# An expert stage that begins with the gather of its first pair alone

## The chip, the cores and the metric

The kernel runs on one core of one Trainium2 chip. The metric is the device time of one execution in microseconds (us); the median of a few runs counts. The core's engines are TensorE (PE; its weight loads are listed apart, as PEld), the vector engine (DVE), the scalar engine (ACT), GpSimd (POOL) and the sync engine (SP), whose queue issues nearly all loads from device memory.

## What is computed

Two transformer blocks of two layers each, on 256 rows of width 1024, in float32. The change touches the mixture of experts, which ends both layers of the first block. Cut to that:

```python
scores = sigmoid(einsum('nd,de->ne', h, router_w))
biased = (scores + router_bias).reshape(n, N_GROUPS, GROUP_SIZE)
group_sel = argmax(sum(top_k(biased, 2)[0], -1), -1)     # the best of 4 groups
...
_, idx = top_k(cand, TOP_K)                              # 2 of that group's 4 experts
sel = take_along_axis(scores, idx, -1)
gates = sel / sum(sel, -1, keepdims=True)
...
ffn = sum over experts e of gate_e * (silu(h @ w_gate[e]) * (h @ w_up[e])) @ w_down[e]
```

There are 16 experts of inner width 512. Each expert has three weight matrices of 2 MB, so a layer reads some 100 MB of expert weights.

## The kernel before

**Places.** The kernel gives each expert 64 places (`CAP`). After the router it counts for each row the place that it takes in each of its experts, and builds two masks `pm[t]` (one for each half `t` of the rows, 128 x 1024 in float32r): column 64 e + n is one for the row that has place n of expert e. The masks are made in two steps at L1246 to L1252, for experts 0 to 3 first.

**Gather.** `gather(g)` multiplies the rows, split into a high and a low float32r part (`hh`, `hl`), by 256 columns of the masks, that is by four experts or two pairs, and so brings the rows of those experts to their places, transposed: 8 blocks j x 2 halves t x 2 parts = 32 matmuls of 128 x 128 weights and 256 columns (L1284, L1285), two blocks to a PSUM bank, copied out by ACT and DVE (L1286, L1287) to the tile `m0` or `m1`.

**Pairs.** Experts are worked in eight pairs. For a pair, `gate_or_up` (L1315) multiplies its gathered rows by the gate and up weights: 16 plain float32 matmuls for each of the two experts and each of the two products; a plain float32 matmul appears in the trace as two passes. The two experts of a pair write the upper and the lower half of one bank, and run side by side. `act` (L1324, L1325) makes silu(gate) x up x the gate of the place, `tr` (L1331) transposes it behind the next pair's gate products, `down` (L1348) multiplies by the down weights, `scatter` (L1365) adds the result to the rows. Two transposes of short vectors for later layers (L683, L689) come in layer 0 at the start of pair 1.

**Gates of the places.** Before the pairs, 16 small matmuls (32 passes, L1296) bring each row's gate to its place, and two copies (L1300) put them into `gsl`, which `act` reads. Just ahead of them, `memory_gemm` (L1722) uses the waiting time of the router for a product of the second block.

**Banks.** Tiles of PSUM are named by tag: `mm` has three banks, `tp` one, and who takes one waits until the reader of the one before is done. L1296, L1331 and L683 all use `tp`.

**Loads.** `Stream` loads weights in one fixed order on SP's queue, 1 MB at a time, into 7 buffers `stage` and 6 `piece`, and a few free tiles ahead of time. A load is issued when its buffer has been released by the matmuls that read it (L141), and the queue keeps its order, so one load that waits holds up all behind it.

**Order.** Instructions of an engine run in the order in which a scheduler puts them: by the order of the code, moved where `after(...)` says that work is to be placed behind another instruction.

Of the kernel before, what the change touches and what calls it, by code (L numbers as in the profile page):

```python
# [9 lines left out]
F32 = mybir.dt.float32  # L10
F32R = mybir.dt.float32r
I32 = mybir.dt.int32
AF = mybir.ActivationFunctionType
# [3 lines left out]
P = 128  # L17
# [249 lines left out]
class Kern:  # L267
# [911 lines left out]
    def moe(self, l, res, ln):  # L1179
        nc, I, c, ws = self.nc, self.I, self.c, self.ws  # L1180
        n, hh, hl = ln.n, ln.hh, ln.hl
# [3 lines left out]
        p = self.tp()  # L1185
        for t in range(2):
            o = p[:, 16 * t:16 * t + 16]
# [13 lines left out]
        k = 0  # L1201
# [41 lines left out]
        nc.vector.scalar_tensor_tensor(posx, sel, -FAR, pp[:, 0:32], op0=OP.mult, op1=OP.add)  # L1243

        pm = [self.mp.tile([P, D], F32R, name="gv", tag="gv", bufs=2) for t in range(2)]
        for e0, e1 in ((0, 4), (4, 16)):  # L1246
            for t in range(2):
                at_pm = nc.vector.tensor_tensor(
                    pm[t][:, CAP * e0:CAP * e1].rearrange("p (e n) -> p e n", n=CAP),
                    c["slot"][:, None, 0:CAP].to_broadcast([P, e1 - e0, CAP]),  # L1250
                    posx[:, 16 * t + e0:16 * t + e1].rearrange("p (e o) -> p e o", o=1).to_broadcast([P, e1 - e0, CAP]),
                    op=OP.is_equal)  # L1252
        pos = self.sm(48, "gpos")
        nc.vector.tensor_copy(pos, pp[:, 0:48])

        gates = self.sm(32, "ggate")
# [14 lines left out]
        xg = []  # L1271
# [14 lines left out]
                nc.scalar.activation(x[:, j0, :], p[:, 0:256], AF.Copy)  # L1286
                nc.vector.tensor_copy(x[:, j0 + 1, :], p[:, 256:512])  # L1287

        gather(0)
        self.memory_gemm(l, 0, [self.prob()[:, 0:512] for t in range(2)], {7: [at_pp]})  # L1290

        p = self.tp()
        gsl = self.sm(8, "gsl")
        for pr in range(8):
            for t in range(2):
                nc.tensor.matmul(p[:, 2 * pr:2 * pr + 2], pm[t][:, P * pr:P * pr + P].bitcast(F32),  # L1296
                                 gates[:, 16 * t + 2 * pr:16 * t + 2 * pr + 2], start=(t == 0), stop=(t == 1))
        pv = p[:, 0:16].rearrange("p (a k) -> p a k", k=2)
        for k in range(2):
            nc.vector.tensor_copy(gsl[64 * k:64 * k + 64, :], pv[64 * k:64 * k + 64, :, k])  # L1300

        act_t, ptr = [], []

# [66 lines left out]
        state = {}  # L1370
        pend = None
        for pr in range(9):
            if pr == 4:
                more = nc.values_load(ovi[0:1, 0:1], min_val=0, max_val=1)
                with self.tc.If(more > 0):
                    self.moe_more(l, res, pos, gates, hh, hl, act_t[0][:, 1024:2048])
            if pr < 8:
                ga = gate_or_up("gate", pr)
            if pend is not None:
                with self.after(*([state["gate"]] if pr < 8 else [])):  # L1380
                    at = tr(pr - 1, pend)
            if pr == 2:
                ptr.append(self.slot("xl", F32R).rearrange("p (a n) -> p a n", a=8))
                for q in range(0, 8, 2):
                    p = self.mm()
                    for k in range(2):
                        for t in range(2):
                            nc.tensor.transpose(p[:, 256 * k + P * t:256 * k + P * t + P],
                                                pm[t][:, P * (q + k):P * (q + k) + P].bitcast(F32), c["ident"])
                    nc.scalar.activation(ptr[0][:, q:q + 2, :], p.rearrange("p (a n) -> p a n", a=2), AF.Copy)  # L1390
            with self.after(*([state["gate"]] if 1 < pr < 8 else [])):
                if pr in (3, 5):
                    gather(pr // 2 + 1)
                if pr > 1:
                    scatter(pr - 2, y)
            if pr < 8:
                ua = gate_or_up("up", pr)
            if pend is not None:
                y = down(pr - 1, at)
            if pr == 1:  # L1400
                with self.after(state["down"]):
                    gather(1)
            if pr < 8:
                pend = act(pr, ga, ua)
            else:
                nxt = LayerNorm(self, res, gb, ("xh", "xl"), self.gcol["ffn1_norm_2", 0] if l else None)
                scatter(7, y)
            if pr == 6:
                ws.hold("fgn" if l else "w_in")
            if pr == 0 and l == 0:  # L1410
                with self.after(at_act, at_pm):
                    self.gain_columns(1)
                    for _ in self.vectors(1):
                        pass
            if pr == 5:
                rows = self.spread_gb(I["ln2_g"], I["ln2_b"], l, "m2")
                next(rows)
            if pr == 6:
                gb = next(rows)
        m0 = self.slot("m0")  # L1420
# [11 lines left out]
        at = self.memory_gemm(l, 1, [m0[:, 512 * t:512 * t + 512] for t in range(2)], {0: [state["scatter"]]}, first, l)  # L1432
# [842 lines left out]
```

## Time and profile before

| | us |
|---|---|
| median of 3 runs | 1941.78 (1941.69 to 1943.78) |
| the profiled execution | 1940.31 |
| its span | 1938.5 |
| TensorE busy in the span | 1891.8 |
| expert products of layer 0 begin | 177.85 |
| expert products of layer 1 begin | 559.95 |

The span is the profiled execution from its first to its last instruction; all times in rows are counted from its start. In the table by stretches, a line gives the busy time of each engine in that stretch and in brackets the number of its instructions, then TensorE's granted clock (1.00 is full speed), the mean busy share of the 16 DMA engines (it can read slightly over 1) and the GB/s that they moved. In the timeline, a line is an instruction, or several of a kind that follow each other (x count), with start and length. Matmuls overlap, so their lengths don't add up: how long a row of matmuls takes is read from one start to the next.

### The profile page before, as it was taken

Reading aid. Unit: us, or ns where it says so; the run is one execution under the profiler, and the core shown is the slowest. Engines: PE = TensorE matmul, PEld = TensorE weight load, DVE = VectorE, ACT = ScalarE, POOL = GpSimd, SP = SyncE. Lnnn points to the kernel's source line nnn. Section 1 sums busy time; section 2 is a strip of 40 time slices with the busy share of each in tenths; the row PEclk is TensorE's granted clock in tenths of the full one; section 3 lists DMA queues with packets and bytes.
Section 4 is the critical chain, followed back from the end, with each engine's and each line's share of the span. In section 5 each row is a group of like instructions: output and inputs, shape, how many; then the busy total and the mean of one; then the engine's idle time right before and its main releaser. Section 6 shows DMA issues by size and latency. Waiting matters only on the chain.

```text
span 1938.5 us, 27919 instructions
## 1 busy us (share of the span) xinstructions
PE 1891.8 (98%) x11029; PEld 1449.2 (75%) x11029; DVE 1117.4 (58%) x2226; ACT 862.8 (45%) x1550; POOL 46.4 (2%) x93
## 2 busy tenths in 40 slices
PE   6999999999999999999999999999999999999999
PEld 6775444378754443799988988899899986788998
DVE  6875122277741223765579857555655568766554
ACT  5662111056521101654477656544644466656443
POOL 1010000000000000000001000000000000000000
PEclk9999999999999999999999999999999999999999
DMA  8568999964679999655553553555555553434550
GB/s 284 174 232 297 399 426 426 423 235 157 236 305 414 425 426 422 235 187 211 181 185 110 175 217 131 194 179 183 195 174 196 195 164 135 152 109 157 192 196 23
DMA packets 175211, 453.36 MB, mean 234 GB/s; under 512 B 10288, under 2 KB 106012, under 8 KB 148316
## 3 DMA queue, kind: packets, MB, share of 16 engines
q1 hardware_dynamic: 171212, 435.53, 60.2%
q0 software_dynamic: 3856, 15.91, 2.4%
q8 instruction: 91, 1.49, 0.3%
q14 instruction: 52, 0.43, 0.1%
HBM read 446.17 MB, written 5.24 MB: 233 GB/s over the span
## 4 chain that ended last, share of the span: by engine, by line
PE 60%; ACT 2%; DMA 2%; DVE 2%; issue 0%; POOL 0%; ACTq 0%; SPq 0%
PE mm L1588 8%; PE mm L1589 8%; PE mm L1587 8%; PE acca L487 5%; PE acca L488 5%; PE accb L486 4%; PE accb L487 4%; PE accb L488 4%; PE acca L486 4%; PE mm L1315 2%; DMA piece<-in_exp_w_down_dram 1%; DMA piece<-in_exp_w_gate_dram 1%; PE mm L1851 1%; PE acca L1348 1%; PE accb L1348 1%; PE mm L545 1%
## 5 line engine op out<-in xcount | busy, mean ns | idle before, releaser
L167 DVE TENSOR_TENSOR piece<-stage,piece 128x1024 fp32r<-128x1024 f32 (+3 forms) x439 | 513.5, 1179 | 238.2 <-ACT piece L166 236.6
L166 ACT ACTIVATE piece<-stage 128x1024 fp32r<-128x1024 f32 (+3 forms) x439 | 444.1, 1022 | 335.8 <-PE mm L1589 198.3
L1315 PE MATMUL mm<-stage,m 128*64 128x512 f32 x528 | 225.1, 595 | 2.4 <-DMA stage<-in_exp_w_gate_dram 2.4
L1315 PE MATMUL mm<-piece,m 128*64 128x512 f32 x480 | 213.4, 595 | 2.6 <-DMA piece<-in_exp_w_gate_dram 2.5
L1588 PE MATMUL mm<-m,piece 128*128 128x256 f32 x736 | 206.6, 281 | 0.0
L1587 PE MATMUL mm<-m,piece 128*128 128x256 f32 x736 | 206.2, 280 | 0.0
L1589 PE MATMUL mm<-m,piece 128*128 128x256 f32 x736 | 206.1, 280 | 0.0
L1587 PE MATMUL mm<-xh,piece 128*128 128x256 f32 x576 | 163.1, 283 | 0.0
L1589 PE MATMUL mm<-xh,piece 128*128 128x256 f32 x576 | 163.0, 283 | 0.0
L1588 PE MATMUL mm<-xl,piece 128*128 128x256 f32 x576 | 162.9, 283 | 0.0
L486 PE MATMUL accb<-piece,m 128*128 128x512 f32 (+1 forms) x364 | 143.2, 394 | 1.4 <-DVE res L1670 0.8
L487 PE MATMUL accb<-piece,m 128*128 128x512 f32 (+1 forms) x364 | 144.4, 397 | 0.0
L488 PE MATMUL accb<-piece,m 128*128 128x512 f32 (+1 forms) x364 | 144.2, 396 | 0.0
L1587 PEld LDWEIGHTS mm<-m,piece 128*128 128x128 f32 x736 | 138.4, 188 | 1.9 <-issue 0.3
L1588 PEld LDWEIGHTS mm<-m,piece 128*128 128x128 f32 x736 | 138.2, 188 | 1.6 <-issue 0.2
L1589 PEld LDWEIGHTS mm<-m,piece 128*128 128x128 f32 x736 | 138.7, 189 | 0.2 <-issue 0.2
L486 PE MATMUL acca<-piece,m 128*128 128x512 f32 (+1 forms) x348 | 137.3, 396 | 0.9 <-ACT m L496 0.8
L487 PE MATMUL acca<-piece,m 128*128 128x512 f32 (+1 forms) x348 | 137.8, 396 | 0.0
L488 PE MATMUL acca<-piece,m 128*128 128x512 f32 (+1 forms) x348 | 137.3, 395 | 0.0
L1315 PEld LDWEIGHTS mm<-stage,m 128*64 128x64 f32 x528 | 67.7, 137 | 82.9 <-issue 74.8
L1587 PEld LDWEIGHTS mm<-xh,piece 128*128 128x128 f32 x576 | 110.4, 192 | 1.3
L1588 PEld LDWEIGHTS mm<-xl,piece 128*128 128x128 f32 x576 | 110.4, 192 | 1.2
(572 smaller groups left out, 3480.2 us busy)
## 6 DMA issues: line engine op xcount, KB each, us to landing
stage<-in_ffn_wi_dram SPq DMA_DIRECT2D x88, 1024.0 KB, 5.1
stage<-in_ffn_wo_dram SPq DMA_DIRECT2D x44, 1024.0 KB, 5.1
stage<-in_exp_w_gate_dram SPq DMA_DIRECT2D x34, 1024.0 KB, 12.5
stage<-in_exp_w_down_dram SPq DMA_DIRECT2D x34, 1024.0 KB, 13.0
stage<-in_exp_w_up_dram SPq DMA_DIRECT2D x32, 1024.0 KB, 13.0
piece<-in_exp_w_gate_dram SPq DMA_DIRECT2D x30, 1024.0 KB, 10.6
piece<-in_exp_w_up_dram SPq DMA_DIRECT2D x30, 1024.0 KB, 11.0
piece<-in_exp_w_down_dram SPq DMA_DIRECT2D x24, 1024.0 KB, 19.5
```

The source lines that it names most:

```text
L166: nc.scalar.activation(wh, src, AF.Copy)
L167: nc.vector.tensor_tensor(wl, src, wh.bitcast(F32), op=OP.subtract)
L486: nc.tensor.matmul(out, ah, bh, start=first, stop=False)
L487: nc.tensor.matmul(out, ah, bl, start=False, stop=False)
L488: self.last_mm = nc.tensor.matmul(out, al, bh, start=False, stop=last)
L545: self.moved = nc.tensor.transpose(p[:, k * P:(k + 1) * P], src[:, 4 * q + k:D:8], self.c["ident"])
L1315: mm = nc.tensor.matmul(o[64 * k:64 * k + 64, :], x[:, j, s:s + CAP], w[k][:, jj, :], start=(j == 0), stop=(j == 7))
L1348: prev[:] = [nc.tensor.matmul(y[nb][64 * k:64 * k + 64, :], x[:, f, 64 * k:64 * k + 64], w[k][:, cc, nb * 512:(nb + 1) * 512], start=(f == ...
L1587: nc.tensor.matmul(out, wh[:, j, :], hi[:, j, :], start=(j == 0), stop=False)
L1588: nc.tensor.matmul(out, wh[:, j, :], lo[:, j, :], start=False, stop=False)
L1589: nc.tensor.matmul(out, wl[:, j, :], hi[:, j, :], start=False, stop=(j == 7))
L1851: nc.tensor.matmul(po[:, k * P:(k + 1) * P], v[:, mc, h * 256 + cc * P:h * 256 + (cc + 1) * P], pt[t][:, (2 * h + mc) * P:(2 * h + mc + 1) ...
```

## The change

The masks are made for the first pair alone (experts 0 and 1), then for all others behind the copies of the first gather. The first gather takes 128 columns, for one pair: the new `gather_pair(q)` fills one half of `m0`, with four blocks j to a bank. The other half and the gates of the places follow behind the up products of pair 0. Later gathers are as they were.

```diff
-        for e0, e1 in ((0, 4), (4, 16)):
+        def places(e0, e1):
             for t in range(2):
...
+        at_pm = places(0, 2)
...
-        gather(0)
+        def gather_pair(q):
+            if not xg:
+                xg.append(self.slot("m0").rearrange("p (j n) -> p j n", j=8))
+            x = xg[0][:, :, P * q:P * q + P]
+            for j0 in range(0, 8, 4):
+                p = self.mm()
+                for j in range(j0, j0 + 4):
+                    o = p[:, P * (j - j0):P * (j - j0) + P]
+                    for t in range(2):
+                        m = pm[t][:, P * q:P * q + P]
+                        nc.tensor.matmul(o, hh[:, t, j, :], m, start=(t == 0), stop=False)
+                        nc.tensor.matmul(o, hl[:, t, j, :], m, start=False, stop=(t == 1))
+                p4 = p.rearrange("p (j n) -> p j n", j=4)
+                nc.scalar.activation(x[:, j0:j0 + 2, :], p4[:, 0:2], AF.Copy)
+                at = nc.vector.tensor_copy(x[:, j0 + 2:j0 + 4, :], p4[:, 2:4])
+            return at
+
+        at_x = gather_pair(0)
+        with self.after(at_x):
+            at_pm = places(2, 16)
         self.memory_gemm(l, 0, [self.prob()[:, 0:512] for t in range(2)], {7: [at_pp]})
...
+        def place_gates():
+            p = self.tp()
...
             if pr < 8:
                 ua = gate_or_up("up", pr)
+            if pr == 0:
+                with self.after(state["up"]):
+                    gather_pair(1)
+                    place_gates()
```

On TensorE, layer 0, from the last matmuls of the memory (L1722) to the start of pair 1, before. `gv` are the masks, `m_1665` and `m_1666` the split rows, `m_1746` the gathered rows:

```order
L1722 MATMUL acca<-piece,m_1438 128x512
L1284 MATMUL mm<-gv,m_1665 128x256
L1285 MATMUL mm<-gv,m_1666 128x256
...
L1722 MATMUL acca<-piece,m_1438 128x512 x2
L1296 MATMUL tp<-ggate,gv 128x2 x16
L1315 MATMUL mm<-stage,m_1746 64x512
...
L683 MATMUL tp<-ident,w_1900 128x84
L1315 MATMUL mm<-piece,m_1746 64x512
```

The same stretch now. In the changed kernel the lines of the gather are L1304 and L1305, of the gates L1322, of the expert products L1341:

```order
L1752 MATMUL acca<-piece,m_1438 128x512
L1304 MATMUL mm<-gv,m_1665 128x128
L1305 MATMUL mm<-gv,m_1666 128x128
...
L1752 MATMUL acca<-piece,m_1438 128x512 x2
L1341 MATMUL mm<-stage,m_1744 64x512
L1341 MATMUL mm<-piece,m_1744 64x512
...
L1322 MATMUL tp<-ggate,gv 128x2 x16
L1341 MATMUL mm<-piece,m_1744 64x512
L683 MATMUL tp<-ident,w_1932 128x84
```

Pair 0's products now stand straight behind the memory product; behind the last of them come 32 more rows of L1304 and L1305, then the gates, and one matmul of pair 1 ahead of the transpose L683.

On the vector engine, the same place before. `mm_...` are the banks of the gather (L1287) and of pair 0's up products (`mm_1868`), `tp_1823` the bank of the gates:

```order
L686 COPY w256_1900<-ssdd_1911 8x128
L1287 COPY m0_1746<-mm_1769 128x256
L1287 COPY m0_1746<-mm_1780 128x256
L1300 COPY gsl_1824<-tp_1823 64x8 x2
L1325 SCALAR_TENSOR_TENSOR prob_1891<-mm_1868,gsl_1824,prob_1891 128x512
L684 COPY vecs1_1899<-tp_1913 128x84
```

And now, with L1308 for the copy of the gather, L1326 for that of the gates and L1351 for the product with the gates:

```order
L1249 TENSOR_TENSOR gv_1727<-blob_75,gposx_1724 128x896
L686 COPY w256_1932<-ssdd_1943 8x128
L1308 COPY m0_1744<-mm_1866 128x2x128
L1326 COPY gsl_1817<-tp_1904 64x8
L1308 COPY m0_1744<-mm_1885 128x2x128
L1326 COPY gsl_1817<-tp_1904 64x8
L1351 SCALAR_TENSOR_TENSOR prob_1923<-mm_1843,gsl_1817,prob_1923 128x512
L684 COPY vecs1_1931<-tp_1945 128x84
```

A copy of the second gather now stands between the two copies of the gates. In layer 1 the rows are the same, without L683 and L684. The queue's loads keep their order.

## Rows read from the trace of the kernel before

**Rows 1.** The page, its head: the span, and the busy time of TensorE.

```profile
span 1938.5 us, 27919 instructions
...
PE 1891.8 (98%) x11029; PEld 1449.2 (75%) x11029; DVE 1117.4 (58%) x2226; ACT 862.8 (45%) x1550; POOL 46.4 (2%) x93
```

**Rows 2.** Busy time by stretches, layer 0; the first line names the columns.

```profile
core 0: us, PE busy (x) PEld busy (x) DVE busy (x) ACT busy (x) POOL busy (x), PEclk, DMA share, GB/s
170.00:176.00 6.00, 6.00 (x44) 5.04 (x43) 2.58 (x9) 2.91 (x6) 1.07 (x2) 1.00 0.40 37
...
180.00:183.00 3.00, 3.00 (x16) 1.01 (x14) 0.00 (x0) 0.00 (x0) 0.00 (x0) 1.00 0.52 135
...
222.00:224.00 2.00, 2.00 (x12) 0.65 (x10) 0.00 (x0) 0.00 (x0) 0.00 (x0) 1.00 0.69 197
...
234.00:236.00 2.00, 2.00 (x12) 0.67 (x10) 0.00 (x0) 0.00 (x0) 0.00 (x0) 1.00 0.73 172
236.00:260.00 24.00, 24.00 (x128) 11.54 (x126) 6.91 (x12) 3.32 (x7) 0.00 (x0) 1.00 1.01 424
260.00:390.00 130.00, 124.35 (x566) 49.17 (x563) 29.61 (x47) 12.58 (x22) 4.17 (x12) 1.00 1.01 424
```

**Rows 3.** The same table, layer 1.

```profile
562.00:566.00 4.00, 4.00 (x20) 1.29 (x18) 0.00 (x0) 0.00 (x0) 0.00 (x0) 1.00 0.53 158
...
604.00:614.00 10.00, 10.00 (x56) 5.42 (x54) 3.17 (x5) 2.66 (x5) 0.00 (x0) 1.00 1.01 421
614.00:617.00 3.00, 3.00 (x16) 1.00 (x14) 0.00 (x0) 0.00 (x0) 0.00 (x0) 1.00 0.75 240
617.00:640.00 23.00, 23.00 (x124) 11.21 (x122) 6.91 (x12) 3.32 (x7) 0.00 (x0) 1.00 1.01 427
640.00:772.00 132.00, 125.09 (x569) 51.65 (x566) 29.36 (x47) 12.58 (x22) 3.97 (x5) 1.00 1.01 424
```

**Rows 4.** Timeline of TensorE, layer 0, first gather to pair 0: start, length, instruction.

```profile
168.63 0.39 PE L1284 MATMUL mm<-gv,m 128*128 128x256 f32 x1
...
172.34 0.28 PE L1284 MATMUL mm<-gv,m 128*128 128x256 f32 x1
172.46 0.28 PE L1285 MATMUL mm<-gv,m 128*128 128x256 f32 x1
172.58 1.88 PE L1722 MATMUL acca<-piece,m 128*128 128x512 f32 x4
174.29 3.63 PE L1296 MATMUL tp<-ggate,gv 128*128 128x2 f32 x32
177.85 0.64 PE L1315 MATMUL mm<-stage,m 128*64 128x512 f32 x1
```

**Rows 5.** The same timeline, transposes of the places behind pair 1.

```profile
226.32 1.94 PE L1388 MATMUL mm<-ident,gv 128*128 128x128 f32 x16
228.02 1.17 PE L1365 MATMUL accb<-xh,xl 128*128 128x512 f32 x4
```

**Rows 6.** Timeline of the vector engine (DVE), the same stretch.

```profile
168.16 2.50 DVE L1248 TENSOR_TENSOR gv<-blob,gposx 128x256 fp32r<-128x256 f32 x4
...
172.23 0.42 DVE L1287 COPY m<-mm 128x256 f32<-128x256 f32 x1 [0.35 <-ACT m L1286]
...
177.96 0.34 DVE L1300 COPY gsl<-tp 64x8 f32<-64x8 f32 x2 [4.34 <-PE tp L1296]
```

**Rows 7.** Timeline of the queue that issues loads (SPq), pairs 0 to 2.

```profile
214.83 0.33 SPq L141 DMA_DIRECT2D stage<-in_exp_w_gate_dram  x1
222.40 0.33 SPq L141 DMA_DIRECT2D piece<-in_exp_w_gate_dram  x1
...
226.25 0.44 SPq L141 DMA_DIRECT2D stage<-in_exp_w_up_dram  x1
233.71 0.33 SPq L141 DMA_DIRECT2D piece<-in_exp_w_up_dram  x1
```

**Rows 8.** Waits of that queue, 176 to 236 us: total, times, longest.

```profile
SPq L141 <- PE mm L1315: 41.9, 12, 7.2
```

More of the change, by code (lines that the diff above doesn't have):

```diff
@@ L1245, in moe @@
         pm = [self.mp.tile([P, D], F32R, name="gv", tag="gv", bufs=2) for t in range(2)]
-        for e0, e1 in ((0, 4), (4, 16)):
+        def places(e0, e1):
             for t in range(2):
-                at_pm = nc.vector.tensor_tensor(
+                at = nc.vector.tensor_tensor(
                     pm[t][:, CAP * e0:CAP * e1].rearrange("p (e n) -> p e n", n=CAP),
@@ L1287, in gather @@
                 nc.vector.tensor_copy(x[:, j0 + 1, :], p[:, 256:512])
-        gather(0)
+        def gather_pair(q):
[13 more added lines that the diff above has]
+                at = nc.vector.tensor_copy(x[:, j0 + 2:j0 + 4, :], p4[:, 2:4])
+            return at
+        at_x = gather_pair(0)
+        with self.after(at_x):
+            at_pm = places(2, 16)
         self.memory_gemm(l, 0, [self.prob()[:, 0:512] for t in range(2)], {7: [at_pp]})
-        p = self.tp()
         gsl = self.sm(8, "gsl")
[L1294 to L1300, printed above, removed]
+        def place_gates():
+            p = self.tp()
+            for pr in range(8):
+                for t in range(2):
+                    nc.tensor.matmul(p[:, 2 * pr:2 * pr + 2], pm[t][:, P * pr:P * pr + P].bitcast(F32),
+                                     gates[:, 16 * t + 2 * pr:16 * t + 2 * pr + 2], start=(t == 0), stop=(t == 1))
+            pv = p[:, 0:16].rearrange("p (a k) -> p a k", k=2)
+            for k in range(2):
+                nc.vector.tensor_copy(gsl[64 * k:64 * k + 64, :], pv[64 * k:64 * k + 64, :, k])
         act_t, ptr = [], []
```

## The prediction

> **What bounds the kernel now.** The totals come first [rows 1]: TensorE is busy for 98% of the span, so time can only come from what stands on TensorE, or from what TensorE waits for. The question is which of the two holds in the expert stages, which the change touches (from 177.85 us in layer 0, from 559.95 us in layer 1). For that I read the table by stretches [rows 2, 3]. The reader is to see three things. The granted clock is 1.00 in every stretch, so no term below rests on the clock. The DMA engines are full from 236 to 390 us in layer 0 (share 1.01, 424 GB/s) and from 617 to 772 us in layer 1, and in the late part of those TensorE has idle time: 130 − 124.35 = 5.7 us and 132 − 125.09 = 6.9 us. So late in a stage the loads of expert weights set the pace, not TensorE. But the loads run dry before that: shares of 0.69 at 222 to 224 us and 0.73 at 234 to 236 us, and 0.75 at 614 to 617 us, while TensorE is busy all the time. There the queue that issues loads waits for a buffer: its waits in 176 to 236 us are for the expert matmuls, 41.9 us in 12 waits [rows 8], and its issues stand far apart (214.83, then 222.40; 226.25, then 233.71) [rows 7].
>
> From this follows the rule by which I cost the change. **The last dry spot couples the two.** The load issued at 233.71 us starts when TensorE frees a buffer in the up products of pair 2, and from then on the loads are back to back to the end of the stage. If TensorE reaches those products S us later, that load and all behind it come S us later, and the end of the stage too. What happens to loads before the dry spot doesn't count. In layer 1 the spot at 614 us plays the same part.
>
> **The change, part by part.** So S is TensorE's time from the first gather to the up products of pair 2, after less before.
>
> *First gather.* Before, 32 matmuls of 256 columns run from 168.63 to 172.58 us: 3.95 us, 0.12 us each (172.34, 172.46, 172.58), of which 0.1 is the switch to them [rows 4]. Now there are 32 of 128 columns. No row shows a float32r matmul under 256 columns. Half the columns at the same rate would be 0.06 us. But each still loads 128 x 128 weights, and rows in which only those weights can count stay well over 0.06: 32 passes with two columns each take 177.85 − 174.29 = 3.56 us, 0.111 each [rows 4], and 16 transposes of 128 columns 228.02 − 226.32 = 1.70 us, 0.106 each [rows 5]. I take 0.110, with ends at 0.106 and at 0.120 (no gain from fewer columns). One pair's gather is then 32 x 0.110 + 0.1 = 3.62 us. Halving the columns saves 0.33 us, not half.
>
> *Second gather.* The other pair's 32 matmuls are new work on TensorE behind the up products of pair 0: 3.62 us.
>
> *Gates of the places.* The 32 passes (3.56 us) move from before pair 0 to behind its up products: 0 in S.
>
> So pair 0 starts 0.33 + 3.56 = 3.9 us earlier, and pair 1 starts 2 x 3.62 − 3.95 = 3.3 us later. With 0.106 it is 3.0, with 0.120 it is 3.9. There is nothing on TensorE in this stretch for the extra work to fill: it is busy all the time in every stretch of rows 2 up to 260 us.
>
> *What waits on the moved pieces.* The vector engine copies the gates out of their bank, 0.34 us for both halves, starting 0.11 us after TensorE could go on (177.96 against 177.85) [rows 4, 6]; between the halves now stands one copy of the second gather (a copy of 256 elements takes 0.42 us [rows 6]). In layer 0 TensorE's next but one matmul is a transpose of the vectors at L683 that needs that bank, since `tp` has one buffer. It waits until about 0.11 + 0.34 + 0.42 = 0.9 us after the gates; one expert matmul of 0.43 us runs first, so the stop is 0.5 us (0 to 0.9). Layer 1 has no such transpose. The product with the gates (L1325) moves behind the copies too, but its reader, the transpose of pair 0, stands behind the gate products of pair 1, some 7 us on. The scalar engine's copies of the second gather lie under the gates' passes.
>
> *Places in two steps.* The mask of the places is made for one pair first (128 columns instead of 256), the rest behind the first gather's copies. The first gather starts at 168.63 us behind matmuls of the memory, as now; the rest of the mask, part of what took 2.50 us in all [rows 6], has the 13.9 us of pair 0's expert products beside it, and is ready before the second gather. 0.
>
> *Loads.* No load is added, dropped or put in another order on the queue. The first releases come 3.9 us earlier, since pair 0 does, and fill the idle DMA time at 180 to 183 us (share 0.52) and 562 to 566 us (0.53). By the rule above this is lost again: the queue runs dry earlier and longer before the releases of pair 2.
>
> **Sum.** Layer 0: 3.3 + 0.5 = 3.8 us. Layer 1: 3.3 us. Together 7.1 us slower, with bounds 2 x 3.0 + 0 = 6.0 and 2 x 3.9 + 0.9 = 8.7. The profiled execution took 1940.31 us (span 1938.5, the rest lies around it), so 1947.4 by it; the median of the runs is 1.47 us above that execution, which gives **1948.9 us** (1947.8 to 1950.5 by the bounds).
>
> A rule speaks for less. The rows give 0.106 to 0.111 us for a matmul whose columns don't count [rows 4, 5]. The Trainium skill, page "TensorE: Matmul & The Clock Gate", section "Back-to-back issue gap", states about 81 ns for each matmul in a stream of weight loads and matmuls of 128 columns; by it one pair's gather would be 2.7 us and the sum an estimated 3.4 us, 1945.2. The trace doesn't agree for the operands it shows, which are 4 bytes wide: not one stream of 128 weight columns is faster than 0.106.
>
> **The rivals.**
>
> *Narrow matmuls are cheap.* If a float32r matmul of 128 columns isn't held by its weights, it takes from 0.06 us (half of 0.12) upward. At 0.06 a pair's gather is 2.0 us, pair 1 starts 0.1 us later, and the sum is 0.7 us with the transpose's stop: 1942.5, no change that can be told. It decides below 0.085, where the sum falls under 3.9 us. For it: the 256-column rows are nearly at the rate of their columns. Against it: every row with 128 weight columns. The page's 81 ns above is a case of this rival.
>
> *Narrow matmuls are dear.* If under 256 columns float32r falls to the rate of plain float32, the four passes of two plain matmuls of 512 columns give the price: 1.71 us / 2 / 4 = 0.214 us for 128 columns [rows 4]. A pair's gather is 6.9 us, pair 1 starts 9.9 us later, the sum is 20.4: 1962. Nothing in the trace excludes it, since every float32r matmul here has 256 columns or more; nothing shows it either.
>
> *The loads carry the time (the other side).* If the stage's end hangs on how early the stream of loads gets going, and not on TensorE's releases at pair 2, then the extra matmuls are eaten by TensorE's later waits for weights (5.7 and 6.9 us), and the loads gain the idle DMA time of their start: 0.48 x 3 = 1.4 us and 0.47 x 4 = 1.9 us, 3.3 us in all. That is 1938.5 to 1941.8: not slower. It decides if the queue doesn't run dry before the releases of pair 2, so that a later release delays nothing. Against it: it runs dry at exactly these places already, with TensorE not yet later, and a head start of loads makes the dry spot longer. For it: the spots are short (0.5 and 0.75 us of idle DMA).
>
> **How the numbers follow.** Chances: the forecast 0.65; narrow cheap 0.13; narrow dear 0.11; loads carry the time 0.11. The predicted time is the forecast's, 1948.9 us. The range leaves out the dear case (0.11) and the faster end of the last (0.04), and reaches down over the cheap case and the absorbed one: 1941 to 1952. A measurement of this kernel can tell about 0.2% (3.9 us) from no change. Slower by more: 0.65 + 0.11 = 0.76. Within it: the cheap case and most of the last, 0.13 + 0.07 = 0.20. Faster by more: 0.04.
>
> **What would show it.** In the profile after: expert products start near 174.0 us instead of 177.85; the two narrow gathers take about 3.6 us each (32 matmuls, 0.11 apart); TensorE stops for about half a us at the transpose of the vectors, in layer 0 alone; pair 1's gate products start 3 to 4 us later than now; the DMA share falls to about a half for several us near 220 us and again just before the up products of pair 2, and is full behind that, with the end of the stage 3 to 4 us later. A gather of 2 us or of 7 us breaks the term for it; a stage that ends no later though pair 2 does breaks the rule of the dry spot.

## The result, and the profile after

The changed kernel takes 1954.1 us (median of 5, 1952.12 to 1954.63) against 1941.78: 12.3 us slower, ratio 1.0059 (95% interval 1.0047 to 1.0070). Two more sets of five gave 1.0067 (1.0053 to 1.0081) and 1.0065 (1.0051 to 1.0080). The forecast was 1948.9 and its range ended at 1952. The side was right; 5 us are missing.

The profiled execution took 1953.91 us. The head of its page, beside [rows 1]:

```profile
span 1952.1 us, 28050 instructions
PE 1904.6 (98%) x11093; PEld 1455.4 (75%) x11093; DVE 1118.1 (57%) x2226; ACT 862.8 (44%) x1550; POOL 46.2 (2%) x93
```

TensorE's timeline in layer 0, from the first gather to pair 1, and at the end of the down products of pair 2, beside [rows 4] (L1304 and L1305 are the narrow gather, L1322 the gates, L1341 the expert products, L1374 the down products; in square brackets stands the idle time before a row and what ended it, and PEq, DVEq and SPq are the instruction queues of the engines):

```profile
167.44 0.41 PE L1304 MATMUL mm<-gv,m 128*128 128x128 f32 x1
171.14 1.93 PE L1752 MATMUL acca<-piece,m 128*128 128x512 f32 x4
173.00 0.64 PE L1341 MATMUL mm<-stage,m 128*64 128x512 f32 x1
...
186.89 0.33 PE L1304 MATMUL mm<-gv,m 128*128 128x128 f32 x1
...
190.51 3.68 PE L1322 MATMUL tp<-ggate,gv 128*128 128x2 f32 x32
194.12 1.49 PE L1341 MATMUL mm<-piece,m 128*64 128x512 f32 x2
...
271.61 3.60 PE L1374 MATMUL accb<-stage,m 128*64 128x512 f32 x16
281.24 1.94 PE L1341 MATMUL mm<-piece,m 128*64 128x512 f32 x2 [6.03 <-DVEq L1401]
```

Up to 194 us this is the forecast: the gathers take 171.14 − 167.44 = 3.70 and 190.51 − 186.89 = 3.62 us, the gates 3.61. The last row was not in it: TensorE stops for 6.03 us behind the down products of pair 2.

The table by stretches, layer 0, beside [rows 2] (the third number from the end is the granted clock):

```profile
180.00:183.00 3.00, 3.00 (x18) 1.00 (x16) 0.00 (x0) 1.88 (x2) 0.00 (x0) 1.00 1.02 421
190.00:194.00 4.00, 4.00 (x39) 4.00 (x37) 0.00 (x0) 0.38 (x1) 0.00 (x0) 1.00 1.02 424
194.00:198.00 4.00, 4.00 (x11) 1.25 (x12) 1.66 (x5) 0.00 (x0) 0.00 (x0) 0.58 0.80 336
198.00:200.00 2.00, 2.00 (x11) 0.60 (x9) 0.17 (x1) 0.00 (x0) 0.00 (x0) 0.99 0.02 8
224.00:228.00 4.00, 4.00 (x20) 1.29 (x18) 0.00 (x0) 0.00 (x0) 0.00 (x0) 1.00 0.24 55
...
238.00:240.00 2.00, 2.00 (x12) 0.72 (x10) 0.00 (x0) 0.00 (x0) 0.00 (x0) 1.00 0.66 160
240.00:260.00 20.00, 20.00 (x109) 9.74 (x106) 4.16 (x8) 3.32 (x7) 0.00 (x0) 1.00 1.01 424
...
280.00:288.00 8.00, 6.76 (x18) 2.40 (x20) 0.69 (x1) 0.00 (x0) 0.00 (x0) 0.57 1.01 424
288.00:390.00 102.00, 101.89 (x478) 41.11 (x476) 25.72 (x41) 10.19 (x18) 4.17 (x12) 1.00 1.01 420
```

Layer 1, beside [rows 3]:

```profile
576.00:580.00 4.00, 4.00 (x37) 4.00 (x38) 0.42 (x1) 0.69 (x2) 0.00 (x0) 1.00 1.01 426
580.00:592.00 12.00, 12.00 (x49) 7.45 (x50) 1.41 (x4) 0.07 (x1) 0.00 (x0) 0.57 0.51 212
...
615.00:619.00 4.00, 4.00 (x22) 1.42 (x20) 0.00 (x0) 0.00 (x0) 0.00 (x0) 1.00 0.35 96
628.00:632.00 4.00, 4.00 (x22) 1.41 (x20) 0.00 (x0) 0.00 (x0) 0.00 (x0) 1.00 0.83 270
...
666.00:676.00 10.00, 3.67 (x12) 1.33 (x12) 1.23 (x2) 0.60 (x1) 0.00 (x0) 0.66 1.01 420
676.00:772.00 96.00, 94.75 (x451) 39.07 (x449) 21.86 (x35) 8.99 (x16) 3.96 (x5) 1.00 1.01 426
```

Three things are new against the rows of before. The clock stands at half (1.2 in place of 2.4 GHz) from the gates on, though TensorE is busy all the time: 4 x (1 − 0.58) = 1.7 us lost in layer 0, 12 x (1 − 0.57) = 5.1 us in layer 1 (580 to 592 us, where the fall comes 0.9 us after the gates have begun). It is low again behind the stop at 275 us (8 x 0.43 = 3.4 us at most, since TensorE still stood for the first 1.2 us of it) and behind the one at 666 us. And the waits that TensorE had all along the late part (5.7 and 6.9 us) are gone from there: 101.89 of 102 us are busy behind 288 us in layer 0, 94.75 of 96 behind 676 us in layer 1. The loads' early start is as forecast (share 1.02 where it was 0.52), and so is its end: a share of 0.02 at 198 us and 0.24 at 224 to 228 us.

The queue of loads at pair 2, beside [rows 7]:

```profile
226.51 0.33 SPq L141 DMA_DIRECT2D piece<-in_exp_w_gate_dram  x1
...
230.37 0.38 SPq L141 DMA_DIRECT2D stage<-in_exp_w_up_dram  x1
237.83 0.33 SPq L141 DMA_DIRECT2D piece<-in_exp_w_up_dram  x1
```

The load that closes the last dry spot went from 233.71 to 237.83 us, by 4.1 us; pair 2's up products went from 230.04 to 234.15, by 4.1 us. In layer 1 both moved by 14.4 us, which holds the later end of layer 0 too (the load from 614.28 to 628.64, the up products from 610.60 to 624.96).

The stop is at the branch of the kernel. Ahead of pair 4 it loads a flag (L1374 before, L1400 now) and skips `moe_more`, which is for experts with over 64 rows; every engine makes that branch for itself. The scheduler had put it behind 9 of the 16 down products of pair 2 on TensorE, and on the vector engine ahead of both halves of the split of their result (L493). In the changed kernel it slipped behind all 16, and between the two halves. TensorE at the branch before, the vector engine there now:

```profile
269.79 3.19 PE L1348 MATMUL accb<-stage,m 128*64 128x512 f32 x13 [1.27 <-PEq L1375]
```

```profile
275.03 0.69 DVE L493 TENSOR_TENSOR xh<-accb,xh 128x512 fp32r<-128x512 f32 x1 [5.86 <-ACT xh L492]
281.07 0.69 DVE L493 TENSOR_TENSOR xh<-accb,xh 128x512 fp32r<-128x512 f32 x1 [5.35 <-DVEq L1401]
```

The vector engine needs 5.35 us to get past the branch. Before, it did so while TensorE worked on the down products, and TensorE lost 1.27 us. Now it starts only when they are done. TensorE's own branch is over at 277.4 us; from there it waits for the vector engine.

### The profile page after: what moved, and what is told of

The parts are those of the page before. It is cut to its first block, busy times and chain, and to the rows that moved or that the text cites. A ratio compares the mean times of both kernels' runs of the same rounds, so it can differ in the third digit from the quotient of the medians.

```text
span 1952.1 us, 28050 instructions
## 1 busy us (share of the span) xinstructions
PE 1904.6 (98%) x11093; PEld 1455.4 (75%) x11093; DVE 1118.1 (57%) x2226; ACT 862.8 (44%) x1550; POOL 46.2 (2%) x93
## 4 chain that ended last, share of the span: by engine, by line
PE 77%; DVE 3%; DMA 3%; ACT 3%; issue 1%; SPq 0%; ACTq 0%; DVEq 0%
PE mm L1341 8%; PE mm L1618 8%; PE mm L1619 8%; PE mm L1617 8%; PE accb L487 6%; PE accb L488 5%; PE accb L486 5%; PE acca L488 5%; PE acca L487 5%; PE acca L486 5%; PE acca L1374 2%; PE accb L1374 2%; DMA piece<-in_exp_w_down_dram 2%; PE accb L1752 1%; DMA piece<-in_exp_w_gate_dram 1%; ACT piece L166 1%
## 5 line engine op out<-in xcount | busy, mean ns | idle before, releaser
L1341 PE MATMUL mm<-piece,m 128*64 128x512 f32 x480 | 221.4, 614 | 12.4 <-DMA piece<-in_exp_w_down_dram 6.3
L1341 PE MATMUL mm<-stage,m 128*64 128x512 f32 x528 | 233.1, 609 | 0.0
L1341 PEld LDWEIGHTS mm<-stage,m 128*64 128x64 f32 x528 | 70.1, 140 | 79.3 <-issue 74.0
L1341 PEld LDWEIGHTS mm<-piece,m 128*64 128x64 f32 x480 | 65.4, 141 | 75.2 <-issue 72.9
```

The costliest lines, as they stand in the source:

```text
L1341: mm = nc.tensor.matmul(o[64 * k:64 * k + 64, :], x[:, j, s:s + CAP], w[k][:, jj, :], start=(j == 0), stop=(j == 7))
```

## The experiments

Three readings are worked out for the profiles below. The **delay** of a layer is the time from the first matmul of its first gather to the up products of pair 2, less the same in the kernel before (61.40 and 59.87 us). The **end** is the same up to the last scatter (221.68 and 221.84 us). The **loss** is what the clock cost from the gates on: the length of each stretch there times (1 − granted clock). In some profiles the clock fell while the gates still ran; they are counted too. Layer 0 and layer 1 stand with a slash. Two kernels whose order at pair 2 is another (up2_early, split_up2) have no row.

| kernel | delay | end | loss |
|---|---|---|---|
| before, second profile | 0.0 / 0.0 | 0.8 / 0.0 | 0 / 0 |
| changed | 5.3 / 8.7 | 7.0 / 8.9 | 1.7 / 5.1 |
| changed, second profile | 8.6 / 8.7 | 10.4 / 9.2 | 5.1 / 5.1 |
| changed, third profile | 6.9 / 5.4 | 8.4 / 6.0 | 3.4 / 1.7 |
| gates_first | 8.1 / 6.7 | 8.3 / 7.4 | 3.4 / 1.7 |
| gates_apart | 5.5 / 5.8 | 6.9 / 6.2 | 1.7 / 1.7 |
| gates_late | 1.9 / 2.0 | 0.9 / 1.9 | 1.7 / 1.7 |
| branch_late | 1.7 / 1.7 | 1.2 / 1.7 | 1.7 / 1.7 |
| halves_first | 5.1 / 5.1 | 4.4 / 5.5 | 1.7 / 1.7 |
| branch_up | 8.6 / 5.4 | 8.0 / 6.0 | 5.1 / 1.7 |
| after_up | 8.6 / 5.4 | 7.7 / 5.9 | 5.1 / 1.7 |
| apart_up | 5.4 / 7.3 | 4.5 / 7.3 | 1.7 / 3.4 |
| after_split | 5.1 / 3.6 | 6.2 / 3.9 | 3.4 / 1.7 |
| gates_split | −2.4 / −2.4 | −1.7 / −0.9 | 0 / 0 |

### Where the clock falls: four places for the gates and the gather

**gates_first**: the changed kernel, the gates ahead of pair 0 again.

```diff
+        place_gates()
         act_t, ptr = [], []
...
                     gather_pair(1)
-                    place_gates()
```

> The changed kernel, with the gates of the places back ahead of pair 0; only the gather stays split. Theory A (what lowers the clock is the unbroken run of the second narrow gather and the gates, 3.62 + 3.61 us behind pair 0): the run is broken here, so the granted clock stays at 1.00 from 186 to 200 us and from 575 to 592 us, where the changed kernel has stretches at 0.50. The extra matmuls still delay pair 2 by some 3.6 us in each layer: pair 1 starts 3.6 us after the end of pair 0's products, and the time is 1949 to 1951 us. Rival B (the narrow float32r gather alone lowers the clock): the clock falls to 0.50 behind it here too, and the time stays at 1953 to 1955 us.

1955.0 us, before beside it 1942.71 (ratio 1.0063, 1.0049 to 1.0076). The clock fell at the gates in their old place, 3.4 and 1.7 us, and not behind the second narrow gather (granted 1.00 from 194 to 198 us). The place is not quite the old one: in layer 0 the scheduler put three matmuls of pair 0 between the first passes of the gates, and the fall comes 2 us into the unbroken rest of them. Theory A (the unbroken run) and rival B (the narrow gather) both fail as the whole account: where A has full clock it is full, but it falls earlier; the time lies in B's range for another reason.

**gates_late**: the kernel before, the gates alone moved behind pair 0's up products, the gather whole (the edit is shown against the changed kernel).

```diff
-        at_pm = places(0, 2)
+        places(0, 4)
+        at_pm = places(4, 16)
...
-        at_x = gather_pair(0)
-        with self.after(at_x):
-            at_pm = places(2, 16)
+        gather(0)
...
                 with self.after(state["up"]):
-                    gather_pair(1)
                     place_gates()
```

> The kernel before, with only the gates moved behind the up products of pair 0; the first gather is whole. By theory A a run of 3.56 us is what the kernel before has too, so the clock stays at 1.00, nothing is added on TensorE, and the up products of pair 2 start when they did: 1941.5 to 1943 us; the loads' early start (some 3.6 us earlier) is given back at the dry spots. By rival C (the gates behind plain float32 products lower the clock, whatever stands ahead of them) it falls to 0.50 at 194 and 576 us, and the time is 1945 to 1952 us. If an early start of the loads counted, the time would fall below 1940 us.

1943.16 us against 1942.71, ratio 1.0003 (0.9994 to 1.0012). The early start of the loads shows no gain, as the rule of the dry spot has it. The clock fell, 1.7 us in each layer, as rival C has it, but the time stayed under its 1945 to 1952 us: it is set against a kernel before that loses some of this too (see branch_late).

**gates_apart**: the changed kernel, the gates between the gate and the up products of pair 0.

```diff
+            if pr == 0:
+                with self.after(state["gate"]):
+                    place_gates()
...
                     gather_pair(1)
-                    place_gates()
```

> The changed kernel, with the gates between the gate and the up products of pair 0, and the second narrow gather behind the up products: the same matmuls, but 6.9 us of dense products between the two runs. Theory A: the clock stays at 1.00, the same time as with the gates ahead of pair 0, 1949 to 1951 us. Rivals B and C: it falls, 1953 us or more.

1952.59 us against 1942.71, ratio 1.0047 (1.0033 to 1.0061), between the two forecasts. The clock fell behind the gates (1.7 us in each layer), not behind the gather that came 9 us later. Stretches of it in layer 0; the gates run from 180.6 to 184.3 us:

```profile
180.00:184.00 4.00, 4.00 (x35) 3.40 (x31) 0.00 (x0) 1.88 (x2) 0.00 (x0) 1.00 1.00 397
184.00:188.00 4.00, 4.00 (x14) 1.32 (x15) 0.33 (x2) 0.00 (x0) 0.00 (x0) 0.61 1.01 424
```

**branch_late**: the kernel before, the branch held where the changed kernel has it.

```diff
-                more = nc.values_load(ovi[0:1, 0:1], min_val=0, max_val=1)
-                with self.tc.If(more > 0):
-                    self.moe_more(...)
+                with self.after(state["down"]):
+                    more = nc.values_load(ovi[0:1, 0:1], min_val=0, max_val=1)
+                    with self.tc.If(more > 0):
+                        self.moe_more(...)
```

> The kernel before, with the test for surplus rows (the branch) held behind the last down product of pair 2, which is where the scheduler put it in the changed kernel. In the kernel before TensorE stops 1.27 us there, in the changed one 6.03 us, with the clock at 0.50 for a few us behind it. Theory D (the stop costs time, but mostly eats waits for loads that come later): TensorE stops 6 us at the branch in both layers, its later waits of 5.7 and 6.9 us shrink, and the time grows by 0.5 to 4 us: 1942.3 to 1946. Rival (fully eaten): 1941.3 to 1942.3. Rival (added in full, 4.8 us and 3 us of clock in each layer): 1955 us or more.

1943.19 us against 1942.71, ratio 1.0001 (0.9992 to 1.0010). TensorE stops 6.12 and 6.46 us there, and no cost can be told (−1.6 to +1.9 us): the waits for loads behind it go by about as much. A second finding: up to the branch this kernel has the order of the kernel before, and its clock fell behind the gates, 1.7 us in each layer (gates from 173.5 to 177.0 us):

```profile
172.00:176.00 4.00, 4.00 (x28) 3.09 (x26) 0.42 (x1) 1.72 (x3) 1.09 (x2) 1.00 0.35 49
176.00:180.00 4.00, 4.00 (x20) 1.99 (x22) 0.33 (x2) 0.00 (x0) 0.00 (x0) 0.79 0.92 340
180.00:184.00 4.00, 4.00 (x18) 1.27 (x16) 0.00 (x0) 0.00 (x0) 0.00 (x0) 0.78 0.23 43
```

So it falls in the kernel before too, in some executions. The profile behind the prediction was of one in which it did not. So did a second one, **before_again**, which expected otherwise:

> The kernel before once more. Theory C: its gates are the same 32 passes, and other kernels with the same order there had the clock at 0.50 behind them, so here too it falls in at least one layer in this execution, though it did not in the first profile (mean clock 0.998; other executions 0.995 to 0.999). Rival (only a changed order makes it fall): no stretch under 1.00 behind the gates, again.

1943.17 us against 1942.63 for the same kernel, ratio 1.0005 (0.9996 to 1.0014). In its stretches the clock stays up:

```profile
176.00:180.00 4.00, 4.00 (x28) 2.51 (x29) 0.33 (x2) 0.00 (x0) 0.00 (x0) 1.00 0.85 312
```

But the mean clock of the executions of the kernel before goes from 0.995 to 0.999, and the time with it: 1945.9 us at 0.995 and 1939.5 at 0.998 beside this run.

### The extra gather alone, and the rule in both directions

**halves_first**: the kernel before, with two narrow gathers ahead of pair 0 in place of the whole one.

```diff
-        gather(0)
...
+        gather_pair(0)
+        gather_pair(1)
```

> The kernel before, with the first gather made as two narrow gathers of 128 columns, both ahead of pair 0. Nothing else moves, the branch stays where it was. This is the main term of the prediction alone: two gathers of 3.5 to 3.6 us in place of one of 3.95, so pair 2 comes 3.2 to 3.4 us later in each layer, by the rule of the dry spot the end of each stage too, and the time is 6.5 us above before. Rival (the loads carry the time): the end of the stages does not move with pair 2, and the time is within 2 us of before. How often the clock falls behind the gates is a scatter of 1.7 us each on both.

1950.03 us against 1941.88, ratio 1.0041 (1.0028 to 1.0055): 8.2 us, where 6.5 was expected. The delay is 5.1 us in each layer, of which 1.7 is the clock behind the gates; the 64 narrow matmuls themselves take 7.3 us and run at full clock:

```profile
172.00:176.00 4.00, 4.00 (x33) 3.62 (x32) 1.05 (x3) 0.97 (x3) 0.00 (x0) 1.00 0.00 0
...
180.00:184.00 4.00, 4.00 (x18) 1.71 (x19) 0.33 (x2) 0.00 (x0) 0.00 (x0) 0.71 0.86 311
```

The ends came 4.4 and 5.5 us later: the stage follows pair 2.

**up2_early**: the kernel before, with the transposes of the places and the first scatter behind the up products of pair 2.

```diff
-            if pr == 2:
-                ptr.append(...)
-                ...
-                if pr > 1:
+                if pr > 2:
                     scatter(pr - 2, y)
             if pr < 8:
                 ua = gate_or_up("up", pr)
+            if pr == 2:
+                with self.after(state["up"]):
+                    ptr.append(...)
+                    ...
+                    scatter(0, y)
```

> The kernel before, with the transposes of the places (L1388, 1.70 us) and the first scatter (2.02 us) moved from ahead of the up products of pair 2 to behind them. The same rule the other way: TensorE frees the buffers of pair 2's up products 3.7 us earlier, so the last dry spot closes earlier, all loads behind it come 3.7 us earlier, and the end of each stage too, as far as TensorE's later waits for loads (5.7 and 6.9 us) have room. Rule of the dry spot: 5 to 7.4 us faster, 1935 to 1938 us. Rival (loads carry the time, or TensorE becomes the bound at once): within 2 us of before.

1939.41 us against 1941.88, ratio 0.9981 (0.9972 to 0.9990): faster, but by half of what I expected or less. Its stretches at pair 2 (gate products from 222.5, up products from 230.2 us):

```profile
226.00:229.00 3.00, 3.00 (x16) 1.00 (x14) 0.00 (x0) 0.00 (x0) 0.00 (x0) 1.00 0.72 224
229.00:260.00 31.00, 31.00 (x167) 15.29 (x164) 7.27 (x12) 6.03 (x12) 0.00 (x0) 1.00 1.01 425
```

In layer 0 the dry spot at the up products is gone, and the one ahead of it, at the gate products, has become the last; in layer 1 the loads are full from 600 us on (shares of 1.01 to 1.03). My reading is that what is earlier than the spot ahead buys only the idle time of the spot that it removes, while a delay has no such bound, since it makes the spot longer. The rows don't prove it: the profiled execution, 1941.71 us, is the slowest of eleven, lost 3.4 and 1.7 us of clock at the gates, and its stages end no earlier than before. The forecast of split_up2 below rests on this reading.

### The branch

**branch_up**: the changed kernel, the branch given a higher priority, so that it stands behind 3 of the 16 down products and ahead of the splits.

```diff
-                more = nc.values_load(ovi[0:1, 0:1], min_val=0, max_val=1)
-                with self.tc.If(more > 0):
+                with self.tc.high_priority(60):
+                    more = nc.values_load(ovi[0:1, 0:1], min_val=0, max_val=1)
+                with self.tc.high_priority(60), self.tc.If(more > 0):
```

> The changed kernel, with the branch given a higher priority, so that it stands behind 3 of the 16 down products of pair 2 on TensorE and ahead of the first split on the vector engine, as nearly as could be had to its place in the kernel before (behind 9 of 16). Theory D (the 6 us stop behind the last down product, and 3.4 us of clock behind it, made TensorE the bound to the end of the stage in layer 0): TensorE stops 1 to 2 us there in place of 6, waits for loads again later, and the end of the stage follows pair 2 by the same distance as before (160.3 us in layer 0, 162.0 in layer 1); 1 to 2.5 us faster than the changed kernel, 1951.5 to 1953. Rival (the stop cost nothing, since loads set the pace): the same time as the changed kernel, 1954.

1950.96 us against 1941.88, ratio 1.0044 (1.0031 to 1.0058). The stop is back to its size before, with no fall of the clock behind it:

```profile
275.19 0.61 PE L1374 MATMUL accb<-piece,m 128*64 128x512 f32 x1 [1.66 <-PEq L1402]
```

From pair 2's up products to the end of the stage it is now 159.7 us in layer 0, where the changed kernel has 162.0 (160.3 in the kernel before); in layer 1, 162.6 against 162.2, no gain. The stretch from 288 to 390 us in layer 0 shows why; in this order before, branch_late and branch_up (the changed kernel stands above with 101.89):

```profile
288.00:390.00 102.00, 97.63 (x448) 38.84 (x445) 24.40 (x39) 10.79 (x19) 4.17 (x12) 1.00 1.01 424
288.00:390.00 102.00, 101.77 (x473) 40.28 (x472) 26.26 (x43) 10.79 (x19) 4.17 (x12) 1.00 1.01 425
288.00:390.00 102.00, 98.47 (x455) 41.23 (x456) 25.72 (x41) 10.19 (x18) 4.17 (x12) 1.00 1.01 426
```

With the late branch TensorE never waits for a load again in layer 0, in the changed kernel and in branch_late alike: there the stop has made TensorE the bound. With the early one it does wait, though pair 2 comes 8.6 us later. So a delay of pair 2 does not use up the late waits, and the stop of some 6 us is as long as they are (5.7 us in layer 0). What then decides, as I read it, is how much of the low clock falls behind the restart (half of the time from TensorE's restart to the clock's rise): 1.3 and 1.4 us lost in branch_late and gates_first, where the end comes 0.5 us less and 0.2 us more than the delay; 2.4 to 2.9 us in the other five profiles with the late branch, where it comes 1.1 to 1.9 us later than the delay. That is read from seven profiles; no run changes the clock there alone.

To set the branch against the rest with the control beside it, the changed kernel, this one once more and a third were run together.

> The changed kernel as the control of the next two: 12 to 14.5 us above before.

> The changed kernel with the branch moved up, now beside the changed kernel itself. By the rows (the end of the stage follows pair 2's up products by 161.97 and 162.15 us in layer 0 with the late branch, 159.74 with this one; layer 1 the same within 0.4) the branch costs about 2 us: 2 us under the changed kernel. If the stop of 6 us counted in full it would be 9 us or more, if loads hid it, none.

**apart_up** is gates_apart with the branch moved up in the same way.

> The changed kernel with both undone: the gates between the gate and up products of pair 0, away from the second narrow gather, and the branch moved up. Only the extra gather is left, 3.5 us in each layer, and dips behind the gates of about the size that the kernel before has too: 7 to 8 us above before, so 3 to 5 us under the changed kernel, and 1 to 3 us under after_up. If the dips had nothing to do with the narrow gather ahead of the gates, it would equal after_up.

Before took 1941.73 us, the changed kernel 1954.3, after_up 1952.46 (1.0051, 1.0038 to 1.0065), apart_up 1950.62 (1.0042, 1.0029 to 1.0056). So by the medians the branch costs 1.8 us, the gates straight behind the narrow gather another 1.8, and 8.9 us are left, where 7 to 8 were expected. The intervals of the three ratios overlap; the steps come in the expected order and size, but neither is settled by these times alone. The rows speak for them: the end against the delay for the branch, the loss for the gates.

### The gates, cheaper

**gates_split**: the kernel before, the gates from a high and a low float32r part, 16 single passes of four columns.

```diff
+        nc.vector.tensor_copy(g4[:, :, 0, :], gk)
+        nc.vector.tensor_tensor(g4[:, :, 1, :], gk, g4[:, :, 0, :].bitcast(F32), op=OP.subtract)
...
-                nc.tensor.matmul(p[:, 2 * pr:2 * pr + 2], pm[t][:, P * pr:P * pr + P].bitcast(F32),
-                                 gates[:, 16 * t + 2 * pr:16 * t + 2 * pr + 2], ...)
+                nc.tensor.matmul(p[:, 4 * pr:4 * pr + 4], pm[t][:, P * pr:P * pr + P],
+                                 ghl[:, 32 * t + 4 * pr:32 * t + 4 * pr + 4], ...)
...
-            nc.vector.tensor_copy(gsl[64 * k:64 * k + 64, :], pv[64 * k:64 * k + 64, :, k])
+            nc.vector.tensor_reduce(gsl[64 * k:64 * k + 64, :], pv[64 * k:64 * k + 64, k], axis=AX.X, op=OP.add)
```

> The kernel before, with the gates of the places made from a high and a low float32r part in 16 single passes of four columns, where plain float32 takes 32 passes of two. By the rows with weights of 128 columns (0.111 us each) the gates take 1.8 us in place of 3.56, so all behind them in the stage comes 1.8 us earlier in both layers. With a shorter run of matmuls of few columns, the clock should fall behind it less often. Rule of the dry spot: 3.5 us faster without a dip in either, up to 5 with; 1938 to 1940 us. Rival (the price goes by passes of plain float32, or four columns cost more): no gain.

1935.01 us against 1941.88, ratio 0.9961 (0.9947 to 0.9974): 6.9 us faster, twice the 3.5 expected. TensorE's timeline at the gates (L1302), and the stretch behind them:

```profile
173.61 2.24 PE L1302 MATMUL tp<-gghl,gv 128*128 128x4 f32 x16
175.79 0.64 PE L1321 MATMUL mm<-stage,m 128*64 128x512 f32 x1
```

```profile
174.00:182.00 8.00, 8.00 (x47) 3.96 (x47) 0.54 (x3) 0.69 (x1) 0.55 (x1) 1.00 0.68 214
```

The first of them is recorded beside the last pass of the memory product, 0.43 us ahead of the second, so they take 1.8 us in place of 3.56, as expected; the delay of −2.4 us holds more than that, since two of the four passes of the memory product now stand ahead of the first gather. The clock did not fall behind them in either layer. Two times 1.8 us are half of the gain. The mean granted clock of the executions, 0.9974 against 0.9968, would make some 1.2 us more, and about 2 us stay open: in the profile, 2.0 of the 3.8 us by which its span is shorter lie behind layer 1, where the edit changes nothing.

**after_split**: the changed kernel with these gates.

> The changed kernel, with the gates in 16 single passes of four columns (high and low part), in their new place straight behind the second narrow gather. Theory C (plain float32 passes of two columns set the clock off): no stretch under 1.00 behind the gates, pair 2 comes 1.5 us earlier by the shorter gates and 1.7 to 5 us by the clock, and the time is 1944 to 1948 us; what is left over the kernel with the same gates in its old order (1935) is the extra gather, some 7 us, and the branch, some 2. Rival A (the run of 3.6 us of narrow gather and gates together sets it off): the clock falls here too, 1948 to 1952.

1947.41 us against 1942.63, ratio 1.0024 (1.0015 to 1.0033). Here the clock did fall, 3.4 and 1.7 us, in layer 0 halfway through the 16 passes: straight behind the narrow gather the short gates are not spared either. The theory that only the 32 passes set it off fails in this place, though the time lies in its range.

**after_again** is the changed kernel once more.

> The changed kernel once more, beside the kernel before in the same session. The time: 11 to 13 us above before. Of the clock: in the first profile it was at 0.50 behind the gates for a stretch that lost 1.7 us in layer 0 and 5.1 us in layer 1. If the amount is an accident of the execution (theory C: the 32 passes of two columns set it off, the length varies), other amounts, in steps of 1.7 us, are seen here; if it is fixed by the order of the work, 1.7 and 5.1 again. The stop at the branch (6 us, then 3.4 us of clock) should be the same.

1957.12 us (1952.83 to 1960.37) against 1942.63: 14.5 us, where 11 to 13 were expected. The profiled execution is the slowest, 1960.37, and lost 5.1 us in both layers. The executions of the changed kernel spread over 7.5 us, and the loss behind the gates is what differs most between its profiles.

**split_up2**: gates_split and up2_early together.

> A better version: the kernel before, with the gates in 16 single passes, and the transposes of the places and the first scatter behind the up products of pair 2. The gates gave 6.9 us, the move 2.5 us (3.5 at the same clock). With the move the last dry spot (0.5 and 0.8 us of idle DMA time) is gone and the one ahead of it, at the gate products of pair 2, sets the stream of loads; so the move is worth what was idle at the last spot, 1 to 2 us: 1933 to 1934.5 us. If the full 3.7 us of each layer came through: 1928.

1933.95 us (1932.32 to 1934.93), ratio 0.9954 (0.9940 to 0.9968): 8.7 us faster than before, within the 1933 to 1934.5 expected, and not the 1928 of the full 3.7 us. It is the lowest median of all, but its interval overlaps that of gates_split.

## Why the prediction was wrong, point by point

**The price of the narrow gather was right.** 3.70 and 3.62 us were measured where 3.62 stood; a matmul takes 0.111 us. Both rivals on it (0.06 to 0.081, and 0.214) are out. The Trainium skill's 81 ns for such a stream (page "TensorE: Matmul & The Clock Gate", section "Back-to-back issue gap") does not hold here: the narrow gather in float32r keeps to 111 ns.

**The delay was right, without the clock.** Measured 5.31 and 8.68 us, less losses of 1.7 and 5.1: 3.6 in each layer, 7.2 together, where 3.8 and 3.3 stood. The stop of half a us at the transpose of the vectors did not come: TensorE is busy without a gap from 190 to 200 us. The prediction let one matmul of 0.43 us run ahead of the transpose, but a plain float32 matmul is two passes (L1341 x2 at 194.12 us), 0.86 us at full clock, about as long as the 0.9 us that the prediction gives the copies. Within the 7.2 small items make up for it, in each layer 0.08 us at the first narrow gather and 0.15 at the four passes of the memory product behind it. That the sum without the clock came out so near its 7.1 us is in part luck.

**The rule of the dry spot was right for delays.** In the table, ends differ from delays by −1.0 to +1.9 us over delays from 1.7 to 8.7 (+0.7 and +1.5 in gates_split, where pair 2 comes earlier), and the load at the last dry spot moved by as much as the up products of pair 2. The rival that loads carry the time is out. My use of the same rule for a gain, in the expectation of up2_early, was wrong.

**The step that failed is "the granted clock is 1.00 in every stretch, so no term below rests on the clock".** That was read from one execution. At the gates the clock falls to half in 13 of the 17 profiles taken here, and the time lost there is a delay like any other: a term put at nothing that measured 1.7 + 5.1 = 6.8 us in the changed kernel's first profile. What the change does is to put the narrow gather straight ahead of the gates. In the ten stages profiled in that order with the 32 passes, the clock fell every time, and lost 3.6 us on the mean (1.7 to 5.1). In the eighteen stages with the same passes in another order it lost 1.6 on the mean: nothing in the four of the kernel before, 1.7 in eleven, 3.4 in three. The five losses of 5.1 us all stand among the ten; in them the clock fell 0.9 to 1.1 us after the gates had begun, in the other order never before 2.3 us. The place behind pair 0 is not enough: in gates_late, with the whole gather ahead of pair 0, it costs 1.7 us. That the narrow gather lengthens the loss is shown by these counts; why the clock falls there is not shown.

**A second term was missing: the branch.** The order of the changed kernel showed that it slips by seven down products on TensorE and by one operation on the vector engine, and the prediction said nothing of it, that is, priced it at nothing. Alone its cost can't be told (branch_late). In the changed kernel it is about 2 us, in layer 0: the stop of 6 us uses up the late waits of 5.7 us by itself, and the low clock behind it then counts. In layer 1, with waits of 6.9 us, some 1.4 us of them are left, and no cost shows.

**The sum.** In the first profile: 7.2 (matmuls) + 6.8 (clock) + 1.7 + 0.2 (end beyond delay) = 15.9 us for both stages. The span grew by 13.6, since layer 0 began 1.2 us earlier in this execution (168.6 and 169.2 us in the other two, so not by the change) and the part behind layer 1 took 1.0 us less. Of the medians, 12.6 us in the last comparison, the two undone terms take 1.8 each, and 8.9 are left where the rows give 7.2. The rest, 1.7 us, I put down to the clock behind the gates falling more often than in the kernel before. The mean granted clocks of the executions agree in size (0.9960 for apart_up, 0.9970 for before beside it; a thousandth of 1945 us is 1.9 us), but they don't say where it fell, so that is not shown.

## What to carry to other kernels

One profile shows one execution: before a term is set at nothing because the clock was full, look at how the mean clock and the time of the other executions scatter. Read the whole order of the changed kernel, far behind the edit too, and price what slipped there, a branch above all; a stop that the waits for loads absorb is free only up to their length, and the low clock behind it comes on top. A delay ahead of the last dry spot of a load queue went through in full here; of a gain only a part came through.

## What the runs showed of the hardware that I had not expected

TensorE's clock fell to half without a gap in its work: in the stretch from 194 to 198 us it is busy for 4.00 of 4 us at 0.58, behind 32 passes of two columns. A run of 64 float32r matmuls of 128 columns (7.3 us, halves_first) did not do that, nor did 16 passes of four columns behind a gather of 256 columns (gates_split); behind the narrow gather the clock fell at the same 16 (after_split).

A branch that skips its block costs the vector engine 5.35 us here, and TensorE's queue shows a like size (it stands in the branch for 6.0 us); the scalar engine is past the same branch in 0.4 us. The Trainium skill, page "Runtime: NRT & Kernel Launch", section "Instruction fetch mechanics", says that a taken branch to code outside the fetched pages has to wait for a DMA. It gives no size, and no run here changed the distance of the branch, so whether the 5.35 us are that wait is not shown. How much of it TensorE feels depends on the work queued ahead: 1.0 to 1.8 us with the branch among the down products, 5.9 to 6.5 behind them. In layer 1 of gates_split and of split_up2 a second stop of 4.4 and 3.6 us follows it within 2 us, for which the profile names no release; it stays open.
